# A hybrid attention layer on one core: the seven products of the output projection in another order

## The chip, the cores and the metric

One core of a Trainium2 chip runs the whole kernel. The metric is device microseconds (us) for one execution, as the median of several runs. The engines are called TensorE (PE in the rows; PEld is its weight load), VectorE (DVE), ScalarE (ACT), GpSimd (POOL) and SyncE (SP, here a queue of DMA issues).

## The reference, cut to what matters

The layer normalises 16 meta tokens and 512 real ones, projects them once, runs two attention mixers of 8 heads each (A: grouped queries with rotary positions; B: differential attention), gates both, and projects the concatenated 2048 columns back. What the change touches is the end:

```python
y = jnp.einsum('blc,cd->bld', jnp.concatenate([ya, yb], axis=-1), w_out[layer])
h = h + rmsnorm(y, post_norm_g[layer])
return h[:, N_META:, :]
```

So 512 rows of `y` (2048 inner, 2048 output columns) are made; each row is scaled by the reciprocal root of its mean square, times a gain, and the residual `x` is added.

## The kernel before

Every float32 operand is split into a high part and the rest (`wh` and `wl` for weights, `oh`/`ol`, `uh`/`ul`, `vh`/`vl` for activations), and a product is three matmuls: high by high, rest by high, high by rest. ScalarE makes the high part, VectorE the rest (`wsplit`, `operand`). A weight chunk is 128x1024 float32, loaded into `st` (three buffers), split into `wh`, `wl` (three buffers each). The buffers of a chunk come free when TensorE is through with the chunk three places ahead, so ScalarE and VectorE split at most two chunks ahead of TensorE.

The heads' gated outputs lie transposed in DRAM (`oscr0` to `oscr7`, two heads each; 0 to 3 are mixer B, 4 to 7 mixer A) and, split, in `oh0` to `oh15`. The output projection treats its 2048 columns in quarters of 512. Quarters 0 and 3 are plain (`dense_out`). Quarters 1 and 2 are made as a 2x2x2 block product (rows in halves of two row tiles, inner index in the halves B and A, columns in the two quarters) by Winograd's form of Strassen's scheme, with seven products of half size instead of eight. I number them as the change does:

| product | activations | weights (blocks (column quarter, inner half)) |
|---|---|---|
| one | `oh`, first rows, half B | (0,0) |
| two | `oh`, first rows, half A | (0,1) |
| three | `oh`, last rows, half A | (0,0)+(1,0)+(1,1)+(0,1) |
| four | `t4`: `t2` less first rows of half A | (1,1) |
| five | `t1`: last less first rows of half B | (1,0)+(1,1) |
| six | `t2`: last rows of half A less `t1` | (0,0)+(1,0)+(1,1) |
| seven | `t3`: last rows of half A less those of half B | (0,0)+(1,0) |

Each product is four steps of one weight chunk; a step has 6 matmuls for each of its two row tiles. The last product, four, does step 1 for both row tiles, then steps 2 to 4 for the first, calls `end(0)`, steps 2 to 4 for the second, and calls `end(1)`.

The sums of weights live in four tiles `ch0` to `ch3` (`chain`): a product splits `ch`, and VectorE then adds the next block from `st` (line 700) or SP loads a fresh block over it (line 696). The sums of heads (lines 818 to 835) are made in tiles `ts` from loads of `oscr`; `t1` and `t3` share the buffers `u`, `t2` and `t4` the buffers `v`. The results stand in `y0` to `y3` (row tiles), combined by VectorE as the products end.

When a block of `y` is final, ScalarE squares it into a partial sum `ssy` (line 847) and POOL (line 896) or VectorE (line 970) multiplies it by the gain `gpB`. A row tile's scale `ry` needs all four squares (`ssp` sums three of them on VectorE; POOL adds the fourth and takes the root, lines 928 and 930). A row block then is `y*ry + xr` with `xr` a residual load: fourteen on VectorE (line 939), two on ScalarE and POOL (lines 936, 937), each stored by SP in the order of the code. The order of instructions on each engine is fixed when the kernel is built; every engine works its queue strictly in that order.

Of the kernel before, what the change touches and what calls it, by code (L numbers as in the profile page):

```python
# [108 lines left out]
def kernel(ctx: ExitStack, tc: tile.TileContext, xT, xn, xm, w_s, w_t, w_q, w_o,  # L109
                             gpre, gq, gk, lams, gsub, gpost, ident_d, cos_d, sin_d, dist_d, out):  # L110
    nc = tc.nc
# [8 lines left out]
    pd = ctx.enter_context(tc.tile_pool(name="pd", bufs=4, space=PSUM))  # L120
# [30 lines left out]
    def wsplit(st, c=slice(0, 1024), ws=None):  # L151
        wh, wl = ws or [wp.tile([P, 1024], F32R, name=n, tag=n) for n in ("wh", "wl")]
        with tc.high_priority(rank[0]):
            nc.scalar.activation(wh[:, c], st[:, c], AF.Copy)  # L154
            nc.vector.tensor_tensor(out=wl[:, c], in0=st[:, c], in1=wh[:, c].bitcast(F32),  # L155
                                    op=ALU.subtract)
        return wh, wl
# [34 lines left out]
    todo, chunks = [], []  # L192
# [112 lines left out]
    def hi(dst, src):  # L305
        nc.scalar.activation(dst, src, AF.Copy)  # L306

    def lo(dst, src, h):
        nc.vector.tensor_tensor(out=dst, in0=src, in1=h.bitcast(F32), op=ALU.subtract)  # L309
# [373 lines left out]
    chain = {}  # L683

    def block(r, c, i):
        return w_o[1 + r, :, 8 * c + 2 * i:8 * c + 2 * i + 2, :]

    def plain(r, c):
        return [block(r, c, i) for i in range(4)]

    def summed(add=None, fresh=None):

        def step(i):
            ws = wsplit(chain[i])
            if fresh:
                nc.sync.dma_start(out=chain[i], in_=block(*fresh, i))
            if add:
                st = wp.tile([P, 1024], F32, name="st", tag="st")
                nc.sync.dma_start(out=st, in_=block(*add, i))
                nc.vector.tensor_tensor(out=chain[i], in0=chain[i], in1=st, op=ALU.add)  # L700
            return ws
        return [lambda i=i: step(i) for i in range(4)]

    def whole(g):
        return [w_o[g, :, k0:k0 + 2, :] for k0 in range(0, KT, 2)]

    todo += whole(0) + whole(3) + plain(0, 0) + plain(0, 1) + summed((0, 0)) + summed((0, 1))
    todo += summed((1, 0), fresh=(0, 0)) + summed() + plain(1, 1)

    sc = psc.tile([P, 2, 512], F32, name="sc", tag="sc")  # L710
    pss = dense_T(KEYS, [sc[:, 0, :], sc[:, 1, :]], spread)
# [2 lines left out]
    v = values(pss)  # L714
# [7 lines left out]
    for h in range(NH):  # L722
# [3 lines left out]
        if h + 1 < NH:  # L726
# [3 lines left out]
            v = values(pss)  # L730
# [73 lines left out]
    def operand(tag, i, src):  # L804

        h, l = [yp.tile([P, 2, NP], F32R, name=f"{tag}{x}{i}", tag=f"{tag}{x}{i}") for x in "hl"]
        hi(h, src)
        lo(l, src, h)
        return h, l
# [3 lines left out]
    t1, t2, t3, t4 = [], [], [], []  # L813
# [18 lines left out]
    def fourth_sum(i):  # L832
        a0 = heads_of(4 + i, lo_, nc.sync)
        TTv(out=a0, in0=t2[i][0].bitcast(F32), in1=a0, op=SUB)
        TTv(out=a0, in0=a0, in1=t2[i][1].bitcast(F32), op=ALU.add)
        t4.append(operand("v", i, a0))

    gpB = yp.tile([P, DM], F32, name="gpB")
    nc.sync.dma_start(out=gpB, in_=gpost)
# [14 lines left out]
    def product(ops, pool, beside=None, done=None):  # L854

        pss = [pool.tile([P, 512], F32, name="po", tag="pd") for _ in range(2)]

        def step(u, i, ws):
            wh, wl = ws
            for j in range(2):  # L860
                bh, bl = ops(i, j, u)
                c = slice(j * 512, (j + 1) * 512)
                mm(pss[u], bh, wh[:, c], start=(i + j == 0), stop=False)
                mm(pss[u], bl, wh[:, c], start=False, stop=False)
                mm(pss[u], bh, wl[:, c], start=False, stop=(i + j == 4))

        for i in range(1 if done else 4):
            ws = fetch()
            for u in range(2):
                step(u, i, ws)  # L870
            if beside:
                beside(i)
        if done:
            last = [fetch(len(todo)) for _ in range(3)]
            for u in range(2):
                for i in range(3):
                    step(u, 1 + i, last[i])
# [12 lines left out]
    def C(r, x, u):  # L890
        return y[2 * x + u][:, (1 + r) * 512:(2 + r) * 512]

    def block_done(r, x, u):
        g = 1 + r
        square(2 * x + u, g, C(r, x, u))
        TTp(out=C(r, x, u), in0=C(r, x, u), in1=gpB[:, g * 512:(g + 1) * 512], op=ALU.mult)

    def beside(s):
        if s < 4:
            first_chain(s)  # L900
        if s % 2:
            first_sums(s // 2)
# [2 lines left out]
        collect(0, t, first[t])  # L905
    for t, ps in enumerate(dense_out(3, pd2, beside)):
        collect(3, t, ps)
    for u, ps in enumerate(product(of_y(0, 0), pd)):
        nc.scalar.activation(C(1, 0, u), ps, AF.Copy)
    for u, ps in enumerate(product(of_y(1, 0), pd)):  # L910
        TTv(out=C(0, 0, u), in0=ps, in1=C(1, 0, u), op=ALU.add)
        block_done(0, 0, u)
    for u, ps in enumerate(product(of_t(t1), pd2)):
        nc.scalar.activation(C(1, 1, u), ps, AF.Copy)
    for u, ps in enumerate(product(of_t(t2), pd2, third_sum)):
        TTv(out=C(1, 0, u), in0=ps, in1=C(1, 0, u), op=SUB)
        TTv(out=C(0, 1, u), in0=C(1, 0, u), in1=C(1, 1, u), op=ALU.add)
    for u, ps in enumerate(product(of_y(1, 1), pd)):
        TTv(out=C(0, 1, u), in0=ps, in1=C(0, 1, u), op=SUB)
        block_done(0, 1, u)  # L920
    for u, ps in enumerate(product(of_t(t3), pd, fourth_sum)):
        TTv(out=C(1, 0, u), in0=C(1, 0, u), in1=ps, op=SUB)
        TTv(out=C(1, 1, u), in0=C(1, 0, u), in1=C(1, 1, u), op=ALU.add)
        block_done(1, 1, u)

    def row_scale(t):
        r = yp.tile([P, 1], F32, name="ry", tag="ry", bufs=2)
# [5 lines left out]
    def row_block(t, r, x, g, far=False):  # L933
        v = y[t][:, g * 512:(g + 1) * 512]
        if far:
            nc.scalar.activation(v, v, AF.Copy, scale=r)
            TTp(out=v, in0=v, in1=x, op=ALU.add)
        else:
            nc.vector.scalar_tensor_tensor(out=v, in0=v, scalar=r, in1=x, op0=ALU.mult,  # L939
                                           op1=ALU.add)  # L940
        load(out[t * P:(t + 1) * P, g * 512:(g + 1) * 512], v)

    xl_ = [[yp.tile([P, 1024], F32, name="xr", tag=f"ch{2 * t + n}") for n in range(2)]
           for t in range(2)]
    for t in range(2):
        for n in range(2):
            nc.gpsimd.dma_start(out=xl_[t][n], in_=xn[t * P:(t + 1) * P, n * 1024:(n + 1) * 1024])
    xh_ = [[yp.tile([P, 512], F32, name="xr", tag=f"u{'hl'[t]}{g}") for g in range(4)]
           for t in range(2)]
    for t in range(2):  # L950
        for g in range(4):
            nc.gpsimd.dma_start(out=xh_[t][g], in_=xn[(2 + t) * P:(3 + t) * P,
                                                      g * 512:(g + 1) * 512])
    for t in range(TT):
        nc.vector.tensor_reduce(out=sspart[t], in_=ssy[t][:, 0:3], op=ALU.add, axis=AX.X)
        nc.vector.tensor_scalar(out=sspart[t], in0=sspart[t], scalar1=DM * EPS, scalar2=None,
# [1 line left out]
    with tc.high_priority(AHEAD):  # L958
        for t in range(2):
            r = row_scale(2 + t)  # L960
            for g in range(4):
                row_block(2 + t, r, xh_[t][g], g)

    xs = lambda t, g: xl_[t][g // 2][:, g % 2 * 512:(g % 2 + 1) * 512]
    rs = []

    def end(u, ps):
        TTv(out=C(1, 0, u), in0=C(1, 0, u), in1=ps, op=SUB)
        square(u, 2, C(1, 0, u))
        TTv(out=C(1, 0, u), in0=C(1, 0, u), in1=gpB[:, 1024:1536], op=ALU.mult)  # L970
        if u == 1:
            row_block(0, rs[0], xs(0, 1), 1)
            row_block(0, rs[0], xs(0, 2), 2)
        rs.append(row_scale(u))
        row_block(u, rs[u], xs(u, 0), 0, True)
        for g in ((3,) if u == 0 else (3, 1, 2)):
            row_block(u, rs[u], xs(u, g), g)

    product(of_t(t4), pd2, done=end)

# [58 lines left out]
```

## Time and profile before

| what | value |
|---|---|
| median of 3 runs | 954.63 us (954.1 to 956.75) |
| profiled execution | 955.66 us |
| its span, first to last instruction | 953.9 us |
| mean granted clock of TensorE | 0.990 |
| TensorE busy | 926.4 us (97%) |
| VectorE busy | 584.6 us (61%) |
| ScalarE busy | 482.0 us (51%) |
| POOL busy | 164.0 us (17%) |

The times in the rows are us from the start of the span. The changed part begins at 849 us in VectorE's queue and with the product at 854.77 us on TensorE. Matmuls are pipelined: in the rows each lasts 0.39 us, but they start 0.23 us apart. A row of the timeline gives start, length, engine, line, operation, output and inputs, and in brackets how long the engine had been idle and what ended that.

### The profile page before, as it was taken

The numbers are of one execution on the slowest core, as the hardware profiler recorded it, in microseconds if no ns is written. First come the engines' busy times: TensorE is split into PE (matmuls) and PEld (weight loads), VectorE is DVE, ScalarE is ACT, GpSimd is POOL, SyncE is SP. The second block draws the span as 40 slices with busy tenths as digits, with TensorE's granted clock in tenths as the row PEclk, the third lists the DMA queues.
The fourth block names the chain that finished last, engine by engine and source line by source line (L and its number), as shares of the span: only waits on it lengthen the run. The fifth ranks groups of instructions, "written<-read, shape, count | busy, mean of one in ns | idle before, by whom it ended". The sixth has DMA issues, their size and how long they took to land.

```text
span 953.9 us, 14190 instructions
## 1 busy us (share of the span) xinstructions
PE 926.4 (97%) x5498; PEld 810.8 (85%) x5498; DVE 584.6 (61%) x974; ACT 482.0 (51%) x845; POOL 164.0 (17%) x250
## 2 busy tenths in 40 slices
PE   9999999999999999999999999998999999999983
PEld 8899898989989898998997888886888888888862
DVE  6386576757575574757554274447554662476996
ACT  6664655546464554746552254354555743245531
POOL 0001010101001010101201041226212123201054
PEclk9999999999999999999999999999999999999996
DMA  9742122222223222312223223211222346976785
GB/s 333 260 159 99 67 88 88 79 77 100 76 78 99 82 84 77 100 67 78 89 67 100 89 68 109 67 58 54 80 75 78 128 141 202 292 226 193 232 278 196
DMA packets 40611, 117.16 MB, mean 123 GB/s; under 512 B 4672, under 2 KB 9536, under 8 KB 40416
## 3 DMA queue, kind: packets, MB, share of 16 engines
q1 hardware_dynamic: 37072, 104.71, 33.2%
q0 software_dynamic: 3328, 11.54, 4.1%
q8 instruction: 43, 0.70, 0.3%
q14 instruction: 24, 0.20, 0.1%
q10 hardware_dynamic: 144, 0.01, 0.0%
HBM read 107.85 MB, written 8.39 MB: 122 GB/s over the span
## 4 chain that ended last, share of the span: by engine, by line
PE 84%; DVE 7%; DMA 2%; POOL 2%; ACT 2%; issue 1%; SPq 0%; DVEq 0%; POOLq 0%; ACTq 0%
PE pd L63 54%; PE po L63 14%; PE sc L63 6%; PE pv L63 5%; PE tr L66 5%; DVE wl L155 1%; DVE qn L578 1%; DMA st<-in_w_o_dram 1%; DVE y L939 1%; POOL qn L592 1%; DMA ch<-in_w_o_dram 1%; POOL ssh L241 1%; DMA xns<-in_xn_dram 1%; DMA xs<-in_xT_dram 1%; ACT qn L650 0%
## 5 line engine op out<-in xcount | busy, mean ns | idle before, releaser
L63 PE MATMUL pd<-xh,wh 128*128 128x264 f32 (+1 forms) x992 | 333.3, 336 | 0.0
L63 PE MATMUL pd<-xl,wh 128*128 128x264 f32 (+1 forms) x992 | 324.9, 327 | 0.4 <-DVE xl L180 0.4
L63 PE MATMUL pd<-xh,wl 128*128 128x264 f32 (+1 forms) x992 | 324.9, 328 | 0.4 <-DVE wl L155 0.4
L154 ACT ACTIVATE wh<-st 128x1024 fp32r<-128x1024 f32 (+2 forms) x135 | 139.8, 1038 | 208.3 <-PE pd L63 90.5
L155 DVE TENSOR_TENSOR wl<-st,wh 128x1024 fp32r<-128x1024 f32 (+2 forms) x135 | 161.7, 1198 | 98.9 <-ACT wh L154 97.7
L63 PEld LDWEIGHTS pd<-xh,wl 128*128 128x128 f32 x992 | 186.6, 188 | 17.8 <-DVE wl L155 0.7
L63 PEld LDWEIGHTS pd<-xh,wh 128*128 128x128 f32 x992 | 187.3, 189 | 12.9 <-ACT xh L179 0.2
L63 PEld LDWEIGHTS pd<-xl,wh 128*128 128x128 f32 x992 | 187.5, 189 | 12.0 <-DVE xl L180 0.6
L63 PE MATMUL po<-wh,ol 128*128 128x512 f32 x176 | 69.6, 396 | 0.9 <-DVE ol L309 0.9
L63 PE MATMUL po<-wh,oh 128*128 128x512 f32 x176 | 70.3, 400 | 0.0
L63 PE MATMUL po<-wl,oh 128*128 128x512 f32 x176 | 69.8, 397 | 0.0
L463 ACT ACTIVATE p<-p,mx 128x528 f32<-128x528 f32 x64 | 46.5, 728 | 34.2 <-POOL mx L460 34.0
L453 DVE CUSTOM_DVE_ANT_0 p<-sc,dist 128x528 f32<-128x528 f32 x64 | 44.9, 702 | 24.0 <-PE sc L63 23.5
L309 DVE TENSOR_TENSOR pl<-tr,ph 128x512 fp32r<-128x512 f32 x64 | 43.4, 688 | 16.2 <-ACT ph L306 15.0
L306 ACT ACTIVATE ph<-tr 128x512 fp32r<-128x512 f32 x64 | 37.6, 590 | 30.9 <-PE tr L66 30.6
L63 PE MATMUL pd<-wh,xh 128*128 128x512 f32 x128 | 52.2, 408 | 0.8 <-DVE vf L300 0.8
L66 PE MATMUL tr<-ident,p 128*128 128x128 f32 (+1 forms) x320 | 50.9, 273 | 1.7 <-DVE gA L558 0.9
L63 PE MATMUL pd<-wh,xl 128*128 128x512 f32 x128 | 50.6, 395 | 0.0
L63 PE MATMUL pd<-wl,xh 128*128 128x512 f32 x128 | 50.5, 395 | 0.0
L66 PEld LDWEIGHTS tr<-ident,p 128*128 128x128 f32 (+1 forms) x320 | 37.3, 132 | 13.4 <-DVE gA L558 1.6
L413 POOL TENSOR_SCALAR pm<-pm 32x256 fp32r<-32x256 f32 x32 | 20.1, 627 | 149.7 <-ACT pm L306 145.8
L460 POOL TENSOR_SCALAR mx<-mx 128x2 f32<-128x2 f32 x32 | 12.1, 377 | 196.0 <-DVE mx L453 196.0
(206 smaller groups left out, 1582.6 us busy)
## 6 DMA issues: line engine op xcount, KB each, us to landing
st<-in_w_t_dram SPq DMA_DIRECT2D x82, 512.0 KB, 3.6
st<-in_w_o_dram SPq DMA_DIRECT2D x40, 512.0 KB, 4.3
st<-in_w_q_dram SPq DMA_DIRECT2D x16, 512.0 KB, 3.6
xs<-in_xT_dram SPq DMA_DIRECT2D x16, 264.0 KB, 5.7
xns<-in_xn_dram SPq DMA_DIRECT2D x8, 512.0 KB, 5.3
ch<-in_w_o_dram POOLq DMA_DIRECT2D x8, 512.0 KB, 8.8
out_dram<-y SPq DMA_DIRECT2D x16, 256.0 KB, 2.3
os<-oscr SPq DMA_DIRECT2D x6, 512.0 KB, 3.6
```

Of the source, the lines that this page charges most:

```text
L63: self._add(self.nc.tensor.matmul(out, lhsT, rhs, start=start, stop=stop), us)
L66: self._add(self.nc.tensor.transpose(out, in_, ident), 0.109)
L154: nc.scalar.activation(wh[:, c], st[:, c], AF.Copy)
L155: nc.vector.tensor_tensor(out=wl[:, c], in0=st[:, c], in1=wh[:, c].bitcast(F32), op=ALU.subtract)
L241: nc.gpsimd.tensor_tensor(out=dst, in0=dst, in1=mhalf[:rows, :dst.shape[1]], op=ALU.pow)
L306: nc.scalar.activation(dst, src, AF.Copy)
L309: nc.vector.tensor_tensor(out=dst, in0=src, in1=h.bitcast(F32), op=ALU.subtract)
L413: nc.gpsimd.tensor_scalar(out=pm[32:64], in0=pm[0:32].bitcast(F32), scalar1=1.0, scalar2=1.0, op0=ALU.mult, op1=ALU.mult)
L453: nc.vector.tensor_tensor_reduce(out=two(p), in0=sc[:, :, :HALF], in1=two(dist[:, w0:w0 + NT]), scale=1.0, scalar=-3.0e38, op0=ALU.add, op ...
L460: nc.gpsimd.tensor_scalar(out=mx, in0=mx, scalar1=-0.125, scalar2=1.0, op0=ALU.mult, op1=ALU.mult)
L463: nc.scalar.activation(p2[m], p2[m], AF.Exp, scale=0.125, bias=mx[:, m:m + 1], accum_out=sm[:, m:m + 1])
L578: nc.vector.scalar_tensor_tensor(out=raw[:, i, :], in0=raw[:, i, :], scalar=ss[:rows, i:i + 1], in1=g[:rows], op0=ALU.mult, op1=ALU.mult)
```

## The change

The order becomes five, one, two, seven, six, three, four (before: one, two, five, six, three, seven, four). With it

- `t4` takes the buffers `u` (free once seven is done) instead of `v`;
- the fresh block for the chain is loaded by SP and its second block added by an accumulating DMA of POOL, where VectorE added it;
- the heads' sums for seven (`third_sum`, two loads each) stand beside one and two, those for four (`fourth_sum`) beside six and three;
- six's two uses combine through an extra tile `V`, so that quarter 2 of the last rows is final after six and quarter 1 of them after three;
- residuals of row tiles 2 and 3 go into the chain's tiles, those of 0 and 1 into `v`, all loaded by POOL.

```diff
             if fresh:
                 nc.sync.dma_start(out=chain[i], in_=block(*fresh, i))
-            if add:
+                nc.gpsimd.dma_start(out=chain[i], in_=block(*add, i), accum_op=ALU.add)
+            elif add:
...
-    todo += whole(0) + whole(3) + plain(0, 0) + plain(0, 1) + summed((0, 0)) + summed((0, 1))
-    todo += summed((1, 0), fresh=(0, 0)) + summed() + plain(1, 1)
+    todo += whole(0) + whole(3) + summed((1, 0), fresh=(0, 0)) + plain(0, 0)
+    todo += plain(0, 1) + summed((1, 1)) + summed((0, 1)) + summed() + plain(1, 1)
...
-        t4.append(operand("v", i, a0))
+        t4.append(operand("u", i, a0))
...
+    for u, ps in enumerate(product(of_t(t1), pd)):
+        nc.scalar.activation(C(1, 1, u), ps, AF.Copy)
+    for u, ps in enumerate(product(of_y(0, 0), pd, at({1: 0, 3: 1}, third_sum))):
         nc.scalar.activation(C(1, 0, u), ps, AF.Copy)
-    for u, ps in enumerate(product(of_y(1, 0), pd)):
+    for u, ps in enumerate(product(of_y(1, 0), pd2, at({1: 2, 3: 3}, third_sum))):
         TTv(out=C(0, 0, u), in0=ps, in1=C(1, 0, u), op=ALU.add)
         block_done(0, 0, u)
...
+    for u, ps in enumerate(product(of_t(t3), pd2)):
+        V.append(yp.tile([P, 512], F32, name="V", tag="ts", bufs=6))
+        TTv(out=V[u], in0=ps, in1=C(1, 0, u), op=ALU.add)
+    for u, ps in enumerate(product(of_t(t2), pd, at({1: 0, 3: 1}, fourth_sum))):
+        TTv(out=C(0, 1, u), in0=ps, in1=C(1, 0, u), op=SUB)
+        TTv(out=C(1, 0, u), in0=ps, in1=V[u], op=SUB)
+        TTv(out=C(0, 1, u), in0=C(0, 1, u), in1=C(1, 1, u), op=ALU.add)
+        TTv(out=C(1, 1, u), in0=C(1, 0, u), in1=C(1, 1, u), op=ALU.add)
+        block_done(1, 1, u)
...
+    def beside_last(s):
+        if s in (0, 1):
+            fourth_sum(2 + s)
+        if s == 3:
+            for t in (2, 3):
...
+                    x = yp.tile([P, 1024], F32, name="xr", tag=f"ch{2 * (t - 2) + n}")
...
+    for u, ps in enumerate(product(of_y(1, 1), pd, beside_last)):
         TTv(out=C(0, 1, u), in0=ps, in1=C(0, 1, u), op=SUB)
         block_done(0, 1, u)
-    for u, ps in enumerate(product(of_t(t3), pd, fourth_sum)):
-        TTv(out=C(1, 0, u), in0=C(1, 0, u), in1=ps, op=SUB)
-        TTv(out=C(1, 1, u), in0=C(1, 0, u), in1=C(1, 1, u), op=ALU.add)
-        block_done(1, 1, u)
```

In the changed kernel the lines named above move: 696 stays, 697 is the new accumulating load, 700 becomes 701, 818 to 835 become 819 to 836, 847 is 848, 896 is 897, 928 and 930 are 948 and 950, 936 and 937 are 956 and 957, 939 is 959, 968 and 970 are 982 and 984; 917 to 943 are the combinations of products two to three, 939 and 967 residual loads.

On VectorE, the rows ahead of four's last two weight splits, before:

```order
L922 TENSOR_TENSOR y1_8221<-y1_8221,po_9015 128x512
L923 TENSOR_TENSOR y2_8222<-y0_8220,y2_8222 128x512
L155 TENSOR_TENSOR wl_9185<-st_9182,wh_9184 128x1024
L923 TENSOR_TENSOR y3_8223<-y1_8221,y3_8223 128x512
L939 SCALAR_TENSOR_TENSOR y2_8222<-y2_8222,ry_9158,xr_9134 128x512
L155 TENSOR_TENSOR wl_9203<-st_9200,wh_9202 128x1024
```

and after:

```order
L835 TENSOR_TENSOR ts_9070<-vh3_8556,ts_9070 128x512
L836 TENSOR_TENSOR ts_9046<-ts_9046,vl2_8481 128x512
L836 TENSOR_TENSOR ts_9070<-ts_9070,vl3_8557 128x512
L155 TENSOR_TENSOR wl_9181<-st_9178,wh_9180 128x1024
L309 TENSOR_TENSOR ul2_9051<-ts_9046,uh2_9050 128x512
L309 TENSOR_TENSOR ul3_9075<-ts_9070,uh3_9074 128x512
L155 TENSOR_TENSOR wl_9199<-st_9196,wh_9198 128x1024
L943 TENSOR_TENSOR y2_8222<-po_9028,y2_8222 128x512
L943 TENSOR_TENSOR y3_8223<-po_9029,y3_8223 128x512
L982 TENSOR_TENSOR y0_8220<-y0_8220,po_9176 128x512
```

The combinations of seven left this place; two sums of heads and two operand splits for four came to it, and three's subtraction stands behind four's last split.

On POOL, the queue from the gain products of the last rows on, before:

```order
L896 TENSOR_TENSOR y2_8222<-y2_8222,gpB_8218 128x512
L928 TENSOR_SCALAR ry_9158<-ssy2_8226,ssp2_8230 128x1
L930 TENSOR_TENSOR ry_9158<-ry_9158,mhalf_458 128x1
L896 TENSOR_TENSOR y3_8223<-y3_8223,gpB_8218 128x512
L928 TENSOR_SCALAR ry_9169<-ssy3_8227,ssp3_8231 128x1
```

and after:

```order
L897 TENSOR_TENSOR y2_8222<-y2_8222,gpB_8218 128x512
L897 TENSOR_TENSOR y3_8223<-y3_8223,gpB_8218 128x512
L948 TENSOR_SCALAR ry_9154<-ssy2_8226,ssp2_8230 128x1
L948 TENSOR_SCALAR ry_9165<-ssy3_8227,ssp3_8231 128x1
L950 TENSOR_TENSOR ry_9154<-ry_9154,mhalf_458 128x1
```

The scale of row tile 2 stands behind both products and both sums now.

On SP, the stores at the end, before:

```order
L139 DMA out_0_dram<-y2_8222 128x512 x4
L139 DMA out_0_dram<-y3_8223 128x512 x3
L139 DMA out_0_dram<-y0_8220 128x512 x4
L139 DMA out_0_dram<-y3_8223 128x512
L139 DMA out_0_dram<-y1_8221 128x512 x4
```

and after:

```order
L139 DMA out_0_dram<-y2_8222 128x512 x4
L139 DMA out_0_dram<-y3_8223 128x512
L139 DMA out_0_dram<-y0_8220 128x512 x4
L139 DMA out_0_dram<-y1_8221 128x512 x2
L139 DMA out_0_dram<-y3_8223 128x512
L139 DMA out_0_dram<-y1_8221 128x512
L139 DMA out_0_dram<-y3_8223 128x512
L139 DMA out_0_dram<-y1_8221 128x512
L139 DMA out_0_dram<-y3_8223 128x512
```

Behind the first store of `y1` (the one that waits for POOL's line 957) stand six stores, where three stood.

More of the change, by code (lines that the diff above doesn't have):

```diff
@@ L907, with at @@
         collect(3, t, ps)
-    for u, ps in enumerate(product(of_y(0, 0), pd)):
+    def at(table, what):
+        return lambda s: what(table[s]) if s in table else None
+    for u, ps in enumerate(product(of_t(t1), pd)):
+        nc.scalar.activation(C(1, 1, u), ps, AF.Copy)
+    for u, ps in enumerate(product(of_y(0, 0), pd, at({1: 0, 3: 1}, third_sum))):
         nc.scalar.activation(C(1, 0, u), ps, AF.Copy)
-    for u, ps in enumerate(product(of_y(1, 0), pd)):
+    for u, ps in enumerate(product(of_y(1, 0), pd2, at({1: 2, 3: 3}, third_sum))):
@@ L911 @@
         TTv(out=C(0, 0, u), in0=ps, in1=C(1, 0, u), op=ALU.add)
         block_done(0, 0, u)
[L913 to L918, printed above, removed]
+    V = []
+    for u, ps in enumerate(product(of_t(t3), pd2)):
+        V.append(yp.tile([P, 512], F32, name="V", tag="ts", bufs=6))
+        TTv(out=V[u], in0=ps, in1=C(1, 0, u), op=ALU.add)
@@ new lines @@
+    for u, ps in enumerate(product(of_t(t2), pd, at({1: 0, 3: 1}, fourth_sum))):
[4 more added lines that the diff above has]
+        block_done(1, 1, u)
+    xr = {}
+    def beside_last(s):
[3 more added lines that the diff above has]
+            for t in (2, 3):
+                xr[t] = []
+                for n in range(2):
+                    x = yp.tile([P, 1024], F32, name="xr", tag=f"ch{2 * (t - 2) + n}")
+                    nc.gpsimd.dma_start(out=x, in_=xn[t * P:(t + 1) * P, n * 1024:(n + 1) * 1024])
+                    xr[t] += [x[:, :512], x[:, 512:]]
@@ L941, in row_block @@
         load(out[t * P:(t + 1) * P, g * 512:(g + 1) * 512], v)
-    xl_ = [[yp.tile([P, 1024], F32, name="xr", tag=f"ch{2 * t + n}") for n in range(2)]
-           for t in range(2)]
     for t in range(2):
[L946 to L950, printed above, removed]
+        xr[t] = []
         for g in range(4):
-            nc.gpsimd.dma_start(out=xh_[t][g], in_=xn[(2 + t) * P:(3 + t) * P,
-                                                      g * 512:(g + 1) * 512])
+            x = yp.tile([P, 512], F32, name="xr", tag=f"v{'hl'[t]}{g}")
+            nc.gpsimd.dma_start(out=x, in_=xn[t * P:(t + 1) * P, g * 512:(g + 1) * 512])
+            xr[t].append(x)
     for t in range(TT):
@@ L961 @@
             for g in range(4):
-                row_block(2 + t, r, xh_[t][g], g)
-    xs = lambda t, g: xl_[t][g // 2][:, g % 2 * 512:(g % 2 + 1) * 512]
+                row_block(2 + t, r, xr[2 + t][g], g)
     rs = []
@@ L971, in end @@
         if u == 1:
-            row_block(0, rs[0], xs(0, 1), 1)
-            row_block(0, rs[0], xs(0, 2), 2)
+            row_block(0, rs[0], xr[0][1], 1)
+            row_block(0, rs[0], xr[0][2], 2)
         rs.append(row_scale(u))
-        row_block(u, rs[u], xs(u, 0), 0, True)
+        row_block(u, rs[u], xr[u][0], 0, True)
         for g in ((3,) if u == 0 else (3, 1, 2)):
-            row_block(u, rs[u], xs(u, g), g)
+            row_block(u, rs[u], xr[u][g], g)
     product(of_t(t4), pd2, done=end)
```

## Prediction

> **What bounds the kernel now.** I read the page first, then what TensorE waited for from 800 us on, then the busy time by stretch, then each engine's rows in order of time.
>
> ```profile
> span 953.9 us, 14190 instructions
> PE 926.4 (97%) x5498; PEld 810.8 (85%) x5498; DVE 584.6 (61%) x974; ACT 482.0 (51%) x845; POOL 164.0 (17%) x250
> ```
>
> The page says TensorE. Only the last 100 us are changed, and there the waits and the stretches (us, then busy time of PE, PEld, DVE, ACT, POOL, the clock, the DMA share, GB/s) say more:
>
> ```profile
> PE po L63 <- ACT wh L154: 3.1, 1, 3.1
> PE po L63 <- DVE wl L155: 2.2, 2, 1.1
> ```
>
> ```profile
> 854.00:877.00 23.00, 23.00 (x100) 18.48 (x100) 15.84 (x17) 11.04 (x16) 0.00 (x0) 1.00 0.62 189
> 877.00:899.00 22.00, 22.00 (x99) 18.18 (x98) 22.00 (x23) 14.00 (x21) 4.11 (x2) 1.00 0.61 190
> ...
> 910.00:923.00 13.00, 11.90 (x52) 9.26 (x51) 12.03 (x14) 6.58 (x11) 7.88 (x10) 1.00 0.73 252
> 923.00:933.00 10.00, 5.81 (x25) 4.20 (x24) 8.13 (x16) 3.05 (x6) 4.47 (x7) 0.90 0.82 290
> ```
>
> From 877 to 899 us VectorE is as full as TensorE, after 7.2 idle us in the stretch ahead, and TensorE is idle only after 910. The starts of the products before put its three waits into the last two:
>
> ```profile
> 854.77 0.39 PE L63 MATMUL po<-wh,oh 128*128 128x512 f32 x1
> ...
> 888.07 0.39 PE L63 MATMUL po<-wh,vh 128*128 128x512 f32 x1
> ...
> 898.96 0.39 PE L63 MATMUL po<-wh,oh 128*128 128x512 f32 x1
> ...
> 910.16 0.40 PE L63 MATMUL po<-wh,uh 128*128 128x512 f32 x1
> ...
> 922.67 0.39 PE L63 MATMUL po<-wh,vh 128*128 128x512 f32 x1
> ...
> 932.75 0.79 PE L63 MATMUL po<-wh,vh 128*128 128x512 f32 x1 [3.09 <-ACT wh L154]
> ...
> 937.59 0.46 PE L63 MATMUL po<-wh,vl 128*128 128x512 f32 x1
> ...
> 940.65 0.39 PE L63 MATMUL po<-wl,vh 128*128 128x512 f32 x1
> ```
>
> One starts at 854.77, six at 888.07, three at 898.96, seven at 910.16, four at 922.67. A product on sums takes 10.9 us (888.07 to 898.96), one on `oh` 11.2 (898.96 to 910.16). Four takes 18.4: waits of 1.1 and 3.1, and after the long one eleven matmuls in 4.84 us, 0.44 each instead of 0.23. Behind TensorE's end at 941.0 come 12.9 us of tail, so the end has two owners: the arrival of four's operands, and the row work on VectorE and POOL.
>
> **The change, part by part.** *TensorE* does the same matmuls. Five now starts at 854.77, so seven starts at 854.77 + 10.9 + 2 x 11.2 = 888.07, six at 898.97, three at 909.87, four at 921.07; without a wait it would end at 931.97. Four's first step ends at 923.8, and then the first half of its rows needs step 2 (from 923.8), step 3 (from 925.16) and step 4.
>
> *VectorE's queue* decides whether it gets them. Its rows (start, length):
>
> ```profile
> 872.63 1.22 DVE L155 TENSOR_TENSOR wl<-ch,wh 128x1024 fp32r<-128x1024 f32 x1 [1.58 <-ACT wh L154]
> ...
> 875.43 1.23 DVE L155 TENSOR_TENSOR wl<-ch,wh 128x1024 fp32r<-128x1024 f32 x1 [0.32 <-ACT wh L154]
> ...
> 887.41 1.21 DVE L700 TENSOR_TENSOR ch<-ch,st 128x1024 f32<-128x1024 f32 x1
> 888.55 1.21 DVE L155 TENSOR_TENSOR wl<-ch,wh 128x1024 fp32r<-128x1024 f32 x1
> 889.68 0.68 DVE L309 TENSOR_TENSOR ul<-ts,uh 128x512 fp32r<-128x512 f32 x1
> 890.29 1.21 DVE L700 TENSOR_TENSOR ch<-ch,st 128x1024 f32<-128x1024 f32 x1
> ...
> 915.58 3.49 DVE L834 TENSOR_TENSOR ts<-vh,ts 128x512 f32<-128x512 f32 x2
> ...
> 932.73 1.23 DVE L155 TENSOR_TENSOR wl<-st,wh 128x1024 fp32r<-128x1024 f32 x1 [1.05 <-ACT wh L154]
> ...
> 940.97 1.41 DVE L939 SCALAR_TENSOR_TENSOR y<-y,ry,xr 128x512 f32<-128x512 f32 x2 [0.80 <-POOL ry L930]
> ```
>
> Start to start, a 128x1024 piece costs 1.135 us, a 128x512 piece 0.605, a row block 0.66 (two in 1.41). POOL's rows:
>
> ```profile
> 914.77 3.74 POOL L896 TENSOR_TENSOR y<-y,gpB 128x512 f32<-128x512 f32 x2 [0.59 <-ACT jko L847]
> ...
> 928.12 1.44 POOL L896 TENSOR_TENSOR y<-y,gpB 128x512 f32<-128x512 f32 x1 [3.24 <-ACT jko L847]
> 929.55 0.69 POOL L928 TENSOR_SCALAR ry<-ssy,ssp 128x1 f32<-128x1 f32 x1
> 930.33 0.57 POOL L930 TENSOR_TENSOR ry<-ry,mhalf 128x1 f32<-128x1 f32 x1
> 933.39 1.70 POOL L896 TENSOR_TENSOR y<-y,gpB 128x512 f32<-128x512 f32 x1 [2.49 <-ACT jko L847]
> ...
> 944.25 1.12 POOL L928 TENSOR_SCALAR ry<-ssy,ssp 128x1 f32<-128x1 f32 x1 [0.75 <-DVE y L939]
> ...
> 946.84 1.74 POOL L937 TENSOR_TENSOR y<-y,xr 128x512 f32<-128x512 f32 x1 [0.83 <-ACT y L936]
> ```
>
> Beside the two POOL products at 914.77 VectorE took 3.49 us for two pieces that alone take 1.3 (0.605 and a last 0.68): each POOL product takes 1.1 us out of a full VectorE queue.
>
> The change deletes four chain adds (POOL's accumulating loads do them) and adds two 512 pieces: 4 x 1.135 - 2 x 0.605 = 3.3 us less VectorE work. But it puts it late: the operand splits that stood in 877 to 898 move to 859 to 882, where VectorE has room, while all four sums for four and their splits, formerly half made before 898, now stand between six and four. I count the queue from seven's first `wl`. Five's stood 4.54 us ahead of its product (872.63 against 877.17), so seven's stands at 883.5. Up to four's last `wl` there are 16 weight splits and 8 chain adds, 24 x 1.135 = 27.2; 24 pieces of 512 (two L917, two L922, eight L924 to L927, four sums of two, four splits), 14.5; four tiny ones, 0.6; four POOL products on this queue, one of them half hidden, 3.8; one early wait, 0.4. That is 46.5: four's last `wl` is done at 930.1, 3.9 us earlier than before (933.96), but 4.1 us later than its buffer allows (923.8, plus 1.05 for `wh` and 1.14 for `wl`). The `ul` of step 3 is two pieces and a `wl` earlier, at 928.4. So step 3 waits from about 926.1, when its `uh` comes, to 928.5, and step 4 for its `wl`: together about 3.5 us. No earlier product waits: the tightest is six's first step, whose `wl` is there 1 us ahead.
>
> Does this wait lower the clock? Waits of 1.1 us did not, 3.1 did; 2.4 behind another 0.9 is nearer to 3.1, so I take it that it does: eleven matmuls at 0.44 from 928.5, first half of the rows ready at 933.5 (931.2 at full clock). The Trainium skill ("TensorE: Matmul & The Clock Gate", Part 1) ties the slow clock to an idle window of about 3.4 us. By that rule this wait would leave the clock alone and the sum would be 0.4 us less; the trace does not quite agree, since 3.1 us was enough.
>
> *The tail.* Three's subtraction (L943) now stands behind four's last `wl`, and rows 2 and 3 need it for their scale: L943 ends at 930.8.
>
> ```profile
> 943.07 0.63 ACT L847 ACTIVATE jko<-y 128x512 f32<-128x512 f32 x1 [1.39 <-DVE y L968]
> 943.61 0.19 ACT L847 ACTIVATION_READ_ACCUMULATOR jko<-y 128x1 f32 x1
> 946.04 0.72 ACT L936 ACTIVATE y<-y,ry 128x512 f32<-128x512 f32 x1 [2.24 <-POOL ry L930]
> ```
>
> Square 0.73, 931.6; two POOL products at 1.3 (1.44 less what it waited beside a `wl`), 934.3; at the slow clock L982 of the first half and the partial sums behind it are done at 934.6, so two L948 at 0.69 and the first L950 at 0.57 give the scale of row tile 2 at 936.75. Before, it came at 930.9 and four row blocks were done beside TensorE's stall. L982 of the second half stands behind three row blocks and a product, 2.58 us: 939.3 to 940.0. TensorE is through by 937.6, so its own end no longer counts. Then square (940.85), L956 of row 0, which ScalarE now holds behind that square (941.6), POOL's L957 (943.45), L948 1.12, L950 0.55, L956, L957: 947.8. Behind that store stand six more, where before there were three:
>
> ```profile
> 948.60 1.30 SPq L139 DMA_DIRECT2D out_dram<-y  x3
> 950.00 0.41 SPq L139 DMA_DIRECT2D out_dram<-y  x1
> ```
>
> Four starts in 1.4 us are 0.47 apart: the last starts at 950.7 (VectorE's last block: 936.75 + 14 x 0.66 + 3 x 0.6 + 2 x 1.1 = 950.0, just ahead). Before it started at 950.00 and the span ended 3.9 us later. Sum: 954.6 against 953.9, plus 0.7.
>
> *Loads.* Residuals: eight of twelve go out before 917, the other four by 928, and are used after 936; covered. Chain reloads on SP and POOL have some 15 us; covered; without that cover seven would wait for the first. Four's last weights wait for the buffer of its first, free at 919.9:
>
> ```profile
> 922.69 8.85 DMA st<-in_w_o_dram
> ```
>
> ```profile
> st<-in_w_o_dram SPq DMA_DIRECT2D x5, 512.0 KB, 5.2
> ```
>
> With the median 5.2 they land at 925.1, before ScalarE comes to them at 926.0: no cost. With 8.85, as before, 928.8, and `wh`, `uh`, `ul`, `wl` behind them end at 932.3: 2.2 later.
>
> **Rivals.** *Faster, 950.9 to 951.4:* VectorE is not backed up at four, and `wl` follows `wh` at 926.0; everything behind moves by 4.1 us and the clock holds. For it: 3.3 us less work, and more of it before 882, where there was idle time. Against: 22.00 busy of 22.00 in the stretch that the new order lengthens. From 2.9 us off the 46.5 on it counts as faster.
>
> *Slower, 957.4 to 958.3:* four's last load comes late. For it: that very transfer took 8.85 before, and residual loads still run beside it. Against: most have landed. It decides from about 8.9 us.
>
> *The gain stays in TensorE and the end does not move,* my forecast, has its own bounds: POOL's two products at 1.15 or 1.70 (minus 0.3, plus 0.8), L948 at 1.12 instead of 0.69 twice (plus 0.9), clock (minus 0.4): 954.3 to 957.0.
>
> **Numbers.** The profiled execution took 955.66, 1.0 above the median 954.63; its span plus 0.7 means 955.3 on the median, rounded down to 955.2 for the clock. The measurement tells about 0.3%, 2.9 us. No change 0.50 (951.8 to 957.5; its own range 954.3 to 957.0), faster 0.28, slower 0.22; the range 950.5 to 958.3 takes in both rivals.
>
> **What would show it.** Right: TensorE waits at steps 3 and 4 of four for `ul` and `wl`, VectorE without idle time from 884 to 930, the scale of row tile 2 at 936 to 937, seven stores after the last L957. Wrong: four's `wl` done by 927, or a TensorE wait in seven or six (the chain late), or `wh` waiting for a load.

## The result, and the profile after

The changed kernel took 957.81 us (median of 10 runs, 956.71 to 961.91), the kernel before 955.68 beside it. The ratio is 1.0028 with a 95% interval of 1.0015 to 1.0042: slower by about 2.7 us (the medians alone differ by 2.1), where no change (plus 0.6) was forecast. One of the ten runs of the kernel before was a slow one, 1014.84 us, and is left out of the ratio. The profiled execution took 957.11 us, its span is 955.3 (before 953.9).

The page, then busy time by stretch (columns as before), then what TensorE waited for from 800 us on, all of the changed kernel:

```profile
span 955.3 us, 14190 instructions
PE 923.7 (97%) x5498; PEld 809.1 (85%) x5498; DVE 580.4 (61%) x972; ACT 481.8 (50%) x845; POOL 169.2 (18%) x254
```

```profile
877.00:899.00 22.00, 22.00 (x98) 17.91 (x96) 18.78 (x20) 10.70 (x16) 4.08 (x2) 1.00 0.57 180
899.00:910.00 11.00, 11.00 (x50) 9.12 (x49) 10.97 (x13) 4.68 (x5) 1.69 (x3) 1.00 0.86 286
910.00:923.00 13.00, 13.00 (x58) 10.46 (x57) 13.00 (x19) 7.23 (x11) 7.10 (x6) 1.00 0.87 284
923.00:933.00 10.00, 7.66 (x32) 5.43 (x31) 9.38 (x14) 4.38 (x9) 8.94 (x8) 1.00 0.32 105
```

```profile
PE po L63 <- DVE wl L155: 1.9, 1, 1.9
PE po L63 <- DVE ul L309: 0.4, 1, 0.4
```

TensorE waits 2.3 us in the last products instead of 5.3 and keeps its clock (1.00 from 923 to 933, before 0.90). It is through at 935.4 instead of 941.0. Yet the span is 1.4 longer: the tail behind TensorE grew from 12.9 to 19.9 us. The rows that carry that tail, VectorE first, then POOL:

```profile
925.26 2.38 DVE L309 TENSOR_TENSOR ul<-ts,uh 128x512 fp32r<-128x512 f32 x2
927.57 2.46 DVE L155 TENSOR_TENSOR wl<-st,wh 128x1024 fp32r<-128x1024 f32 x1
929.95 1.27 DVE L943 TENSOR_TENSOR y<-po,y 128x512 f32<-128x512 f32 x2
...
935.14 0.75 DVE L959 SCALAR_TENSOR_TENSOR y<-y,ry,xr 128x512 f32<-128x512 f32 x1 [2.56 <-POOL ry L950]
...
938.33 1.41 DVE L959 SCALAR_TENSOR_TENSOR y<-y,ry,xr 128x512 f32<-128x512 f32 x2
940.54 0.75 DVE L959 SCALAR_TENSOR_TENSOR y<-y,ry,xr 128x512 f32<-128x512 f32 x1 [0.80 <-POOL ry L950]
...
945.69 4.41 DVE L959 SCALAR_TENSOR_TENSOR y<-y,ry,xr 128x512 f32<-128x512 f32 x5 [0.80 <-POOL ry L950]
```

```profile
918.57 8.52 POOL L897 TENSOR_TENSOR y<-y,gpB 128x512 f32<-128x512 f32 x1 [1.81 <-ACT jko L848]
...
934.51 1.12 POOL L950 TENSOR_TENSOR ry<-ry,mhalf 128x1 f32<-128x1 f32 x2
939.27 0.60 POOL L948 TENSOR_SCALAR ry<-ssy,ssp 128x1 f32<-128x1 f32 x1 [3.64 <-ACT jko L848]
...
944.39 0.62 POOL L948 TENSOR_SCALAR ry<-ssy,ssp 128x1 f32<-128x1 f32 x1 [1.39 <-DVE y L959]
```

The scale of row tile 2 comes at 935.1, and VectorE has been idle for 2.56 us. Row 0's scale then starts only at 939.27. The row names ScalarE's square, but row 0's own square was made among three that ScalarE ended at 932.96. `ry` has two buffers, row 0's scale takes the one of row 2, and row 2's fourth block runs from 938.33 to about 939.08. For row 1, whose scale takes the buffer of row 3, the row itself names a VectorE block. VectorE is idle for 0.80 twice behind these two.

### The profile page after: what moved, and what is told of

Its sections match the earlier page's. It is cut to its first block, busy times and chain, and to the rows that moved or that the text cites. A ratio compares the mean times of both kernels' runs of the same rounds, so it can differ in the third digit from the quotient of the medians.

```text
span 955.3 us, 14190 instructions
## 1 busy us (share of the span) xinstructions
PE 923.7 (97%) x5498; PEld 809.1 (85%) x5498; DVE 580.4 (61%) x972; ACT 481.8 (50%) x845; POOL 169.2 (18%) x254
## 4 chain that ended last, share of the span: by engine, by line
PE 87%; DVE 5%; POOL 3%; ACT 2%; issue 1%; DMA 1%; DVEq 0%; SPq 0%; POOLq 0%; ACTq 0%
PE pd L63 57%; PE po L63 16%; PE sc L63 5%; PE pv L63 5%; PE tr L66 4%; DVE wl L155 1%; DVE y L959 1%; POOL qn L592 1%; POOL ssh L241 1%; DMA xs<-in_xT_dram 0%; DMA xns<-in_xm_dram 0%; ACT p L550 0%; PE ss L63 0%; DVE mxA L546 0%; DVE qn L578 0%
## 5 line engine op out<-in xcount | busy, mean ns | idle before, releaser
L66 PEld LDWEIGHTS tr<-ident,p 128*128 128x128 f32 (+1 forms) x320 | 37.2, 131 | 12.9 <-DVE gA L558 1.3
```

What stands on the lines that cost most here:

```text
L66: self._add(self.nc.tensor.transpose(out, in_, ident), 0.109)
```

## Experiments

The unchanged part of the program takes a varying time: one matmul near 750 us (TensorE waits there for an `ol`, ahead of all that changed) starts between 749.0 and 752.9 in the profiles here. Rows of two profiles are therefore compared by their distance from that matmul. "End" is the end of the last store's issue:

```profile
750.17 0.51 PE L63 MATMUL po<-wh,ol 128*128 128x512 f32 x1 [0.94 <-DVE ol L309]
931.71 18.69 SPq L139 DMA_DIRECT2D out_dram<-y  x16
```

```profile
749.73 0.49 PE L63 MATMUL po<-wh,ol 128*128 128x512 f32 x1 [0.94 <-DVE ol L309]
935.92 16.11 SPq L139 DMA_DIRECT2D out_dram<-y  x16
```

For the kernel before (first fence) the end is 931.71 + 18.69 - 750.17 = 200.23; for the changed one 202.30. The table gives the same for all runs, with the stretch from VectorE's first row block (the moment when row 2's scale has come) to the end. Each ratio is to the kernel before, run beside it. A profile is one execution, and its end can differ from the ratio by some 2 us (the kernel before with the new chain ends 3.65 later, and its runs are 0.16%, 1.5 us, slower): which kernel is faster is read from the ratios, where the time goes from the profiles.

| kernel | ratio to before | 95% interval | first block | end | stretch |
|---|---|---|---|---|---|
| before | 1 | | 180.76 | 200.23 | 19.47 |
| changed | 1.0028 | 1.0015 to 1.0042 | 185.41 | 202.30 | 16.89 |
| changed, again | 1.0035 | 1.0024 to 1.0047 | 186.46 | 203.35 | 16.89 |
| changed, four scale buffers | 1.0012 | 1.0000 to 1.0023 | 185.54 | 200.28 | 14.74 |
| changed, one scale buffer | 1.0040 | 1.0025 to 1.0054 | 186.30 | 204.28 | 17.98 |
| before, four scale buffers | 0.9996 | 0.9984 to 1.0008 | 181.47 | 199.61 | 18.14 |
| changed, old chain | 1.0095 | 1.0078 to 1.0112 | 190.86 | 207.75 | 16.89 |
| before, new chain | 1.0016 | 1.0003 to 1.0030 | 183.93 | 203.88 | 19.95 |
| changed, products on VectorE | 1.0008 | 0.9999 to 1.0018 | 184.39 | 200.71 | 16.32 |
| changed, loads on SP | 1.0001 | 0.9992 to 1.0011 | 184.77 | 201.66 | 16.89 |
| changed, loads on SP, four buffers | 0.9980 | 0.9969 to 0.9991 | 183.71 | 198.45 | 14.74 |
| combined | 0.9974 | 0.9962 to 0.9987 | 182.68 | 198.21 | 15.53 |
| combined, not pulled ahead | 0.9971 | 0.9959 to 0.9983 | 184.59 | 197.17 | 12.58 |
| before, mended tail | 0.9983 | 0.9972 to 0.9993 | 180.66 | 198.82 | 18.16 |

**Four scale buffers in the changed kernel.**

```diff
-        r = yp.tile([P, 1], F32, name="ry", tag="ry", bufs=2)
+        r = yp.tile([P, 1], F32, name="ry", tag="ry", bufs=4)
```

> The changed kernel with four buffers instead of two for the scale tile ry; nothing else. Theory A (the end is the row chain on VectorE and POOL, and rows 0 and 1 wait for a scale buffer): the first L948 of row 0 starts about 933 to 934.5 right behind its own square, not at 939.3; row 1's scale comes at about 940 instead of 945.7; VectorE loses its two idle times of 0.8 us; the last store is issued 1.5 to 2 us earlier, span 953.3 to 953.8 against 955.3. Rival B (the end is set by four's late operands, and the scale has slack): scales earlier, end the same within 0.5 us. Rival C (VectorE's 14 row blocks fill the tail anyway): at most 0.8 us.

Its rows (anchor, POOL, VectorE, SP):

```profile
752.58 0.50 PE L63 MATMUL po<-wh,ol 128*128 128x512 f32 x1 [0.93 <-DVE ol L309]
```

```profile
920.87 10.28 POOL L897 TENSOR_TENSOR y<-y,gpB 128x512 f32<-128x512 f32 x1 [1.81 <-ACT jko L848]
931.10 0.59 POOL L967 DMA_DIRECT2D xr<-in_xn_dram  x1
...
932.94 1.62 POOL L967 DMA_DIRECT2D xr<-in_xn_dram  x3
934.58 2.50 POOL L897 TENSOR_TENSOR y<-y,gpB 128x512 f32<-128x512 f32 x2
...
938.62 0.91 POOL L948 TENSOR_SCALAR ry<-ssy,ssp 128x1 f32<-128x1 f32 x1
```

```profile
938.12 0.75 DVE L959 SCALAR_TENSOR_TENSOR y<-y,ry,xr 128x512 f32<-128x512 f32 x1 [5.59 <-POOL ry L950]
...
944.48 7.04 DVE L959 SCALAR_TENSOR_TENSOR y<-y,ry,xr 128x512 f32<-128x512 f32 x9
```

```profile
938.90 13.96 SPq L139 DMA_DIRECT2D out_dram<-y  x16
```

Row 0's scale follows rows 2 and 3 without a wait. From the first block to the end are 14.74 us instead of 16.89: the missing buffers cost 2.15. The span shows none of it (956.2 against an expected 953.3 to 953.8), because in this execution the anchor is 2.85 later. The runs do: 1.0012 against 1.0028, whose interval overlaps, and against 1.0035 of the changed kernel's second set, whose interval does not. Row 0's scale started at 938.62 where 933 to 934.5 was written. The anchor's shift is 2.85 of that, and from the anchor row 2's scale comes as in the changed kernel (185.54 against 185.41). But the rows show a wait that was new: POOL's product, issued at 920.87, takes 10.28 us, and behind it three loads stand ahead of the last two products. That this queue of POOL holds back the scales is called theory P from here on.

**Four scale buffers in the kernel before** (the same edit there).

> The kernel before with four buffers for ry. Theory A: little to gain, since there only row 1 waited for a block (0.75 us at 944.25) while the second half of TensorE's rows came at 942: 0 to 0.8 us off 953.9. If it gains as much as the changed kernel does, the two buffers are a cost of both and do not explain the difference between them.

The ratio, 0.9996, is no change that can be told. Its profile has a stretch 1.3 us shorter behind a first block 0.7 later, so the end moves 0.6. Within that interval the old order may lose up to 1.5 us on two buffers. In the stretch they cost it 1.3, and the new order 2.15.

**One scale buffer in the changed kernel** (`bufs=1`).

> The changed kernel with one scale buffer instead of two: the suspected wait doubled. Distances are taken from TensorE's wait for ol near 750 us, ahead of anything that was changed, to the end of the last store's issue (before 200.2, changed 202.3 and 203.4, changed with four buffers 200.3). Theory A (waits for a free scale buffer set the tail of the changed kernel): the scale of row tile 3 waits for the four blocks of row tile 2, and each later scale for its predecessor's blocks; each step adds square, L948, L950 of about 1.9 us with VectorE idle, so 1 to 3 us over the changed kernel: distance 204 to 206, ratio to before 1.005 to 1.007. Rival C (VectorE's blocks fill the tail, the scale has slack): unchanged, 1.003.

```profile
940.32 0.78 POOL L948 TENSOR_SCALAR ry<-ssy,ssp 128x1 f32<-128x1 f32 x1 [4.14 <-DVE y L959]
...
944.71 0.26 POOL L948 TENSOR_SCALAR ry<-ssy,ssp 128x1 f32<-128x1 f32 x1 [2.97 <-DVE y L959]
```

The rows now name a VectorE block ahead of the scales. The stretch grows to 17.98 and the end is 204.28, inside the forecast: the second halving of the buffers costs 1.1 in the stretch, at the low end of the 1 to 3 expected, and that speaks against rival C. The runs do not settle it: 1.0040 stays below the 1.005 that was written, and cannot be told from the changed kernel's 1.0028 and 1.0035.

**The old refill of the chain in the new order.**

```diff
-                nc.gpsimd.dma_start(out=chain[i], in_=block(*add, i), accum_op=ALU.add)
-            elif add:
+            if add:
```

> The new order of products, but the chain's fresh refill takes its second summand as before: loaded by SP and added on VectorE (four more additions of 1.135 us between 883 and 912). Theory A (VectorE's queue is full from 883 to 930 and everything behind it waits for its end): four's last wl 4.5 us later, at 934.6, and the end 3.5 to 4.5 us later, span 959 to 960. Rival D (operands are late because of loads or POOL, not of VectorE's queue): four's last wl where it was, at 930, and the end within 1 us of 955.3.

The end came 4.4 us later than in the changed kernel's second profile, as written, but not by the way written. TensorE's waits:

```profile
864.68 0.50 PE L63 MATMUL po<-wl,uh 128*128 128x512 f32 x1 [1.68 <-DVE wl L155]
...
874.38 0.50 PE L63 MATMUL po<-wh,oh 128*128 128x512 f32 x1 [1.61 <-ACT wh L154]
875.64 0.50 PE L63 MATMUL po<-wl,oh 128*128 128x512 f32 x1 [0.53 <-DVE wl L155]
```

They lie in five and one, 3.8 us together: the four additions stand between 855 and 872, wait there for their loads (3.74 and 2.83 us), and the weights stand behind them, on VectorE the splits and on SP the loads. From seven's first `wl` to the end of four's last VectorE's queue is as long as without them (890.34 to 934.48 here, 885.99 to 930.13 in the second profile of the changed kernel: 44.14 both). The new order needs the accumulating load: without it the ratio is 1.0095.

**The new refill in the old order** (the reverse edit).

> The old order of products, with the chain's fresh refill by POOL's accumulating load (4.5 us less on VectorE between 877 and 912). Theory A: VectorE comes to the split that frees four's last weight buffer earlier (921.45 before), so that load starts and lands earlier, the 3.1 us stall shrinks, and the end moves 1 to 3 us: span 951 to 953. Rival D: the stall stays 3 us since the load is slow for another reason, end within 0.5 us of 953.9.

A miss: 1.0016 instead of faster. The rows of ScalarE and TensorE:

```profile
911.60 1.06 ACT L154 ACTIVATE wh<-ch 128x1024 fp32r<-128x1024 f32 x1 [7.99 <-DMA ch<-in_w_o_dram]
...
934.62 1.06 ACT L154 ACTIVATE wh<-st 128x1024 fp32r<-128x1024 f32 x1 [3.85 <-DMA st<-in_w_o_dram]
```

```profile
935.73 0.50 PE L63 MATMUL po<-wh,vh 128*128 128x512 f32 x1 [1.73 <-ACT wh L154]
```

```profile
PE po L63 <- ACT wh L154: 3.8, 3, 1.7
PE po L63 <- DVE wl L155: 2.6, 5, 0.5
```

In the old order three's refill is used by seven, the very next product, and two loads in a row, the second waiting for the first, are not there in time; in the new order one and two lie between. Seven, which starts at 912.71, waits some 4.1 us in all, where it waited 1.1 before. The stall for four's last load shrank, as theory A has it, from 3.1 to 1.7, but that is less than seven lost. So neither the new order nor the new refill is a gain by itself.

**Products of rows 2 and 3 on VectorE.**

```diff
-        TTp(out=C(r, x, u), in0=C(r, x, u), ...
+        (TTv if x else TTp)(out=C(r, x, u), in0=C(r, x, u), ...
```

> The changed kernel with the four gain products of rows 2 and 3 (L897) on VectorE instead of POOL. Theory P (the step that costs is POOL's queue: its product is starved by VectorE's back-to-back rows, from 918.57 to 927 in the changed kernel's profile and to 931 in the one with four scale buffers, and three loads, three products and the scale of row 2 stand behind it in order): VectorE takes four pieces of 0.605 more and loses the 2.3 us that two products took from it; four's last wl is done about 929, the scale of row tile 2 comes at 933 to 934 instead of 935.1 (or 938 where the product starved to the end), and the span is 953.3 to 954.3, about 0.2 to 0.4% under the changed kernel. Rival A (VectorE's amount of work alone sets the end, POOL is beside the path): VectorE does 2.4 us more, so the end is the same or up to 1.2 us later than 955.3.

The changed kernel ran once more beside it:

> The changed kernel unaltered, on the chip of the other three. Theory P: the starved product ends either at VectorE's first gap (about 931, as with four buffers or the old chain) or earlier by luck (926 in the first profile); where it starves to the end, the scale of row tile 2 comes near 938 and the span is 956 to 957; the ratio to before is 1.002 to 1.004 again. Rival A: the product's length differs and the span does not follow it.

That second profile of the changed kernel, POOL and VectorE:

```profile
921.01 10.27 POOL L897 TENSOR_TENSOR y<-y,gpB 128x512 f32<-128x512 f32 x1 [1.81 <-ACT jko L848]
```

```profile
928.91 1.22 DVE L155 TENSOR_TENSOR wl<-st,wh 128x1024 fp32r<-128x1024 f32 x1
930.05 1.28 DVE L943 TENSOR_TENSOR y<-po,y 128x512 f32<-128x512 f32 x2
...
938.28 0.75 DVE L959 SCALAR_TENSOR_TENSOR y<-y,ry,xr 128x512 f32<-128x512 f32 x1 [5.60 <-POOL ry L950]
```

Here the product does not get in until VectorE is through with four's operands; VectorE loses nothing, and the scale is 1.05 later than in the first profile (186.46 against 185.41). With the products on VectorE the scale comes 2.1 earlier (184.39) and the end 2.6, and the ratio falls from 1.0035 to 1.0008, with 2.4 us more work on the engine that is full: theory P, not the amount of VectorE's work.

**L967's loads issued by SP** instead of POOL.

> The changed kernel with the eight residual loads of rows 0 and 1 (L967) issued by SP, which is idle there, instead of POOL. Theory P: three of them stood between POOL's products, 1.6 to 2.2 us ahead of the scale of row tile 2; the scale comes that much earlier, span 953.5 to 954.8, 0.1 to 0.2% under the changed kernel. Rival A: POOL is beside the path, no change within 0.5 us. A cost that could show: four's last weight load now stands behind four of these loads on SP; if one of them waits, four's wh comes late and TensorE waits over 2 us.

```profile
920.45 14.04 POOL L897 TENSOR_TENSOR y<-y,gpB 128x512 f32<-128x512 f32 x4 [1.82 <-ACT jko L848]
934.48 0.51 POOL L948 TENSOR_SCALAR ry<-ssy,ssp 128x1 f32<-128x1 f32 x2
```

The four products now stand together and the scale comes at 184.77, 1.7 before the second profile; 1.0001. The end is 1.7 earlier too, 0.18%, as expected; the runs gained 0.34% (1.0035 to 1.0001), and what the rest is stays open. TensorE waits 0.42 for four's `ul`, 0.3 for a `wl` and for no `wh`, so SP's queue cost nothing there.

**Loads on SP and four buffers together.**

> The changed kernel with four scale buffers and L967's loads on SP, the two edits that each came out near 1.001 and 1.000. If the two waits are separate pieces of the tail (buffers: between row 2's scale and the last block; POOL's queue: ahead of row 2's scale), the gains add: distance 200.3 less 1.6 to 2.2, 198.1 to 198.7, ratio to before 0.997 to 0.9985. If they are one and the same wait seen twice: 200 to 201, ratio 1.000.

1.0001 becomes 0.9980, with intervals that do not overlap, and the stretch is 14.74 again, where 16.89 was: the two waits are separate, and add. This pair is the cleanest measure of the buffers, 0.21% or 2.0 us.

**All of it combined**, with three's subtraction pulled ahead:

```diff
-        TTv(out=C(0, 1, u), in0=ps, in1=C(0, 1, u), op=SUB)
-        block_done(0, 1, u)
+        with tc.high_priority(50):
+            TTv(out=C(0, 1, u), in0=ps, in1=C(0, 1, u), op=SUB)
+            block_done(0, 1, u)
...
-        row_block(u, rs[u], xr[u][0], 0, True)
+        if u == 0:
+            row_block(u, rs[u], xr[u][0], 0, True)
         for g in ((3,) if u == 0 else (3, 1, 2)):
             row_block(u, rs[u], xr[u][g], g)
+        if u:
+            row_block(u, rs[u], xr[u][0], 0, True)
```

> The changed kernel with everything that theory P and the buffers suggest: products of rows 2 and 3 on VectorE, L967's loads on SP, four scale buffers, three's subtraction and its square and product pulled ahead of the last weight splits, and the store of row 1's ScalarE and POOL block issued last. Theory P: the scales of rows 2 and 3 are there before VectorE is through with four's operands, so it has no idle time in the tail: it works from 931 on for 14 row blocks and 4 pieces (9.3 + 2.4 + 0.1), ends about 943.5 to 946, TensorE ends 1 to 2 us later than 935.4, and the span is 949 to 951.5: faster than both kernels, by 0.3 to 0.5% against before. Rival A: at most 1 us under 955.3.

> The combined version without the edit that pulls three's subtraction ahead of the last weight splits: products of rows 2 and 3 on VectorE, loads on SP, four buffers, row 1's far store last. Theory A/P: row 2's scale comes at about 934 instead of 932.4, and TensorE ends at 934.5 instead of 938.8, so the pull may cost as much as it gives: distance 198 to 199.5 against 198.2 of the combined version, ratio 0.997 to 0.9985. If the place of L943 in VectorE's queue is the cause that matters, it is 1 us or more slower than with the pull (0.999 or above).

The ratio is 0.9974 with the pull and 0.9971 without: 0.26 and 0.29% faster than the kernel before, and the first some 0.6% faster than the changed one beside it (1.0035). The gain with the pull is just under the 0.3% written; TensorE ended 3.6 later instead of 1 to 2, and VectorE, expected without idle time in the tail, still waited four times, 0.44 to 1.19 us. The pull is worth nothing that can be told: it brings row 2's scale 1.9 earlier (182.68 against 184.59), and TensorE is through later, at 939.0 (189.2 us from the anchor, 185.7 in the changed kernel). What the place of L943 in VectorE's queue costs by itself, these two runs do not separate.

**The kernel before with four buffers and row 1's far store last.**

> The kernel before with four scale buffers and row 1's far store last: the same mending of the tail, as far as it applies to the old order. Theory A: the old order has little to mend (four buffers alone gave 0.9996); the last store no longer stands behind POOL's L957, so 0.3 to 1.2 us off: ratio 0.9985 to 0.9996. If it comes down to 0.9974 like the combined version, the new order brings nothing of its own.

0.9983, a little more than expected. Against the combined 0.9971 the new order is ahead by 0.1%, with intervals that overlap: whether it brings anything of its own stays open. More than half of what the combined kernel gains over the kernel before (0.17 of 0.29%) comes from edits of the tail that the old order can have too.

## Why the prediction was wrong

The times written go by the profile of the kernel before, whose anchor lies 0.44 later than that of the changed kernel: from the anchor, four and VectorE's queue start 0.5 us later than written.

**TensorE.** Right: four starts at 921.09 (921.07 was written), and waits for the `ul` of step 3 and the `wl` of step 4. They came to 2.3 us, not 3.5, and the clock held; the term had no weight, since TensorE's end does not count in the tail. The rule of the Trainium skill ("TensorE: Matmul & The Clock Gate", Part 1) that was weighed there gave the clock rightly in this kernel, and not in the combined one (last section).

**VectorE's queue.** Right in the first profile, 883.54 to 930.03 (883.5 to 930.1 written), and term by term: POOL's four products took 3.8 us from it, as written. Two of them lengthen two additions:

```profile
889.87 1.73 POOL L897 TENSOR_TENSOR y<-y,gpB 128x512 f32<-128x512 f32 x1 [23.22 <-ACT jko L848]
892.61 2.35 POOL L897 TENSOR_TENSOR y<-y,gpB 128x512 f32<-128x512 f32 x1 [1.01 <-ACT jko L848]
```

```profile
890.96 1.72 DVE L701 TENSOR_TENSOR ch<-ch,st 128x1024 f32<-128x1024 f32 x1
...
893.74 0.21 DVE L970 TENSOR_REDUCE ssp<-ssy 128x1 f32<-128x3 f32 x2
893.87 2.18 DVE L701 TENSOR_TENSOR ch<-ch,st 128x1024 f32<-128x1024 f32 x1
```

An addition alone lasts 1.22, so these two lost 1.46; the rows at 925.26 and 927.57 lost 2.34 to the other two. In the second profile the first two cost the same and the other two nothing, and the queue is 44.14 long instead of 46.49. In the five further profiles of the new order with these products on POOL the third one waits as it does there, so it was luck that the term for POOL held in the first.

**Row 2's scale.** Written 936.75, which is 186.58 from the anchor (the terms listed for it add up to 936.55); 185.41 and 186.46 measured. Right in size, and in the second profile by two errors that cancel: VectorE is through with four's operands 1.6 us earlier than written (178.31 from the anchor, not 179.93), and POOL takes that much longer from there. The price of a POOL product was wrong in kind: not 1.3 each, but one whose row lasts up to 10.3 us, with four loads and three products in order behind it.

**The step that failed** is the tail from there on, from "L982 of the second half" to "947.8". The prediction took row 0's and row 1's scale as free to start when their squares were done. It read the rows on what each scale is computed from, and not `bufs=2` in the line that allocates its tile. From row 2's scale to the end it wrote 936.75 to 950.7 plus 0.4 for the issue, 14.35. Measured: 16.89 with two buffers in the four profiles of the new order whose products stand on POOL, 14.74 with four buffers in both profiles that have them. The missing term is 2.15 us. Added to the 0.7 that was written it makes 2.9, or 0.30%, against 0.28 and 0.35% measured; and with four buffers the changed kernel comes to 1.0012, which cannot be told from the 0.7 us (0.07%) of the forecast. In the first profile the earlier scale hides 1.2 us of it. Nothing in the profile before priced this wait at more than 0.75: with rows 2 and 3 done beside TensorE's stall, only row 1's scale had a block named ahead of it (944.25).

**The stores.** Right in number: seven leave behind the last L957, which ended at 948.2 (947.8 written), and the last starts at 951.4 instead of 950.7.

**The signs.** Those named for being right nearly all came: the waits for `ul` and `wl`, the full queue, the seven stores, and the scale of row tile 2 (185.4 and 186.5 from the anchor, where 185.8 to 186.8 was written). None of them looked at the tail between that scale and the stores, where the error was.

**The rivals.** The faster one needed VectorE not backed up; from 899 to 923 it was busy 23.97 of 24 us. The slower one, four's last load late, did not come: no wait of TensorE for a `wh` there. What made it slower was a wait that no rival named. The range, 950.5 to 958.3, held the time, and 957.81 even lies in the slower rival's own 957.4 to 958.3, for another cause: that is luck.

## What to carry to other kernels

When work is moved so that several short results come due at once, count the buffers of every small tile they pass through: two cost nothing that the runs could tell while the rows came one by one, and 2.15 us when four were due together. A product on POOL beside a full VectorE queue has no fixed price: here it cost VectorE 0.5 to 1.2 us, or waited 9 us itself, and everything behind it on POOL, loads too, waited with it. In this kernel it paid to give the product to VectorE (0.27%) or the loads to an idle queue (0.34%). A change that ends TensorE 5.6 us earlier is worth only what the tail behind it can take up: measure the tail from its first block to the last store.

## What the runs showed of the hardware

POOL's product got through when VectorE came to an instruction that does not read two tiles in SBUF, as the ends of its rows show. In four profiles of the new order its row ends 1.23 to 1.25 us behind the start of L943, which reads `po` in PSUM (second profile of the changed kernel: 930.05 and 931.28; four buffers: 929.90 and 931.15). That is a product's own length (2.50 for two). Until then VectorE had run pieces with both inputs in SBUF back to back for some 9 us. The early product of the changed kernel that starts at 892.61 ends 1.22 behind VectorE's start on the small sums of L970, which read one tile (893.74).

In the first profile two products got in ahead of L943, and VectorE paid: 2.38 for two pieces that take 1.28, 2.46 for one of 1.22. ScalarE's `uh` for the second of those two pieces was ready only at 925.93, where VectorE, back to back, would have started on it at 925.86. That POOL used this pause fits its row (it ends at 927.09, and 1.25 before that is 925.84), but no run shows it.

The Trainium skill ("SBUF — State Buffer", section "SBUF: two separate sides") says that of a VectorE instruction with two SBUF inputs and a GpSimd one the first to start holds the shared ports and the other blocks fully. The trace agrees, and shows beyond it that a queue of such pieces keeps the other out from piece to piece, for 9.0 of the 10.27 us of its row.

The clock of TensorE fell in the combined version without any wait as long as the 3.1 us of the kernel before:

```profile
926.10 0.50 PE L63 MATMUL po<-wh,uh 128*128 128x512 f32 x1 [1.19 <-ACT uh L306]
926.91 0.49 PE L63 MATMUL po<-wh,ul 128*128 128x512 f32 x1 [0.31 <-DVE ul L309]
928.64 0.50 PE L63 MATMUL po<-wl,uh 128*128 128x512 f32 x1 [1.24 <-DVE wl L155]
...
929.91 0.80 PE L63 MATMUL po<-wh,uh 128*128 128x512 f32 x1
...
931.57 0.63 PE L63 MATMUL po<-wl,uh 128*128 128x512 f32 x1
932.00 0.63 PE L63 MATMUL po<-wh,uh 128*128 128x512 f32 x1
```

Three waits of 1.24 at most, 2.7 together within 3.7 us, and from 929.9 the matmuls are longer and start 0.43 apart instead of 0.23; the granted clock is 0.50 from 930 to 936 us. In the changed kernel 0.41 and 1.89 within 4.5 us left the clock at 1.00, and so did 1.73 and 0.53 within 3 us in the old order with the new refill. Ahead of the 3.1 us of the kernel before stood another wait, of 1.1 (it ends at 928.47). One profile of each does not settle where the line lies.
